# V stage of the expert layer: token-major products, the residual added by identity products

## The chip, the cores and the metric

One core of a Trainium2 chip runs the whole program. The metric is the device time of one execution in microseconds (us), and the number given for a kernel is the median of its runs. One execution is also recorded by the hardware profiler; its span runs from the first to the last instruction on the core.

## The reference

One inference step of one trunk layer, for 512 prompt tokens (with 16 meta tokens ahead of them) and 64 sample tokens: token mixers, then a layer of single-neuron experts (PEER), then a final norm. The part that matters here:

```python
qh = jnp.einsum('td,de->te', xb, w_query).reshape(PEER_BLOCK, PEER_HEADS, 2, KEY_HALF)
s = jnp.einsum('thpd,hpnd->thpn', qh, sub_keys).astype(jnp.float32)
...
gate = jax.nn.softmax(top_s, axis=-1).astype(xb.dtype)
act = jax.nn.gelu(jnp.einsum('thkd,td->thk', expert_u[eidx], xb), approximate=False)
return jnp.einsum('thk,thkd->td', gate * act, expert_v[eidx])
...
h = h + peer(rms_norm(h, norm_ffn), ...)
y = rms_norm(h, norm_final)
```

D = 1024 features, 128 x 128 = 16384 experts, 8 heads, 16 experts for each head and token.

## The kernel before

The program has three long parts: the token mixers (to about 680 us), the routing and the **U stage** (`scored`, `hidden`), and the **V stage** (`experts`). Of the 576 tokens, the last 192 are served by gathers (`gather_begin`, `gather`: GpSimd fetches one row of U or V for each of 128 tokens, VectorE takes the dot product or adds the weighted row). The first `ND` = 384 tokens are served densely: every expert is computed for them. The gathers run through the U stage and most of the V stage, in the same program order as the dense work.

The dense work goes by **halves**. A half is 128 experts. For each one SyncE loads a 512 KB tile of weights (`fetch`, seven halves ahead), ScalarE makes its rounded copy (`hi`, three halves ahead, tiles `uh`), VectorE the remainder (`lo`, two halves ahead, tiles `ul`), and TensorE makes three products per 128 x 128 block (`mm3`: rounded by rounded, rounded weights by remainder, remainder by rounded). In the U stage the product goes through Gelu and most of it is spilled to memory (`gz`). In the V stage two halves (one k) are prepared together, one k ahead: VectorE multiplies the reloaded `gz` by the gate weights `wj` (L1494), ScalarE rounds it (`ah`, L1496), and one half later VectorE makes the remainder (`al`, L1501, called from `run_due`). SyncE also loads `gz` three k ahead and `wj` in slices (`gates`).

The V stage has 128 halves. In one half TensorE takes the eight blocks d of 128 output features in turn. For a block the stationary operand is a 128 x 128 piece of the weights and the moving one is `ah` or `al`, 384 tokens wide, so the output is **feature-major**: eight banks `py[d]`, 128 features x 384 tokens (L1522 and L1523), 24 matmuls of 384 columns in a half. The order of instructions on TensorE, VectorE, ScalarE and SyncE is the order of the program from L1259 on (`in_order`).

After the first 32 halves of the V stage, which use hidden tiles kept in SBUF, the final gain (`gf`) and the residual (`yr`, eight tiles of 128 features x 384 tokens) are loaded (L1542 to L1544). The last two halves run block by block (L1551 to L1554). Behind each block VectorE adds the residual (L1555), ScalarE squares (L1558), VectorE sums the squares (L1557). Then comes the final norm: products with a column of ones (L1564) give the sum over features for each token, `rms_cols` gives the inverse root and spreads it over the partitions by products (L217), ScalarE copies it (L1567), six blocks are scaled by VectorE (L1575) and two by ScalarE and GpSimd (L1572, L1573), and eight stores of 128 rows go out from SyncE and ScalarE (L1576). Gathered tokens are normed token-major in `gather_out` and stored to `yg`.

Of the kernel before, what the change touches and what calls it, by code (L numbers as in the profile page):

```python
# [22 lines left out]
P = 128  # L23
# [25 lines left out]
NG = P + NX  # L49
ND = NT - NG  # L50
SEGD = [(0, ND)]
HB = PH // XG
TBLK = [(ND - P, P), (0, P), (P, P)]
# [67 lines left out]
class Net:  # L121
# [108 lines left out]
    def build(self):  # L230
        tc, nc, I, O = self.tc, self.nc, self.I, self.O
        self.right = ExitStack()
        with self.pool("const") as cp, self.pool("wraw", 3) as self.wraw, self.pool("whl", 2) as self.whl, \
# [5 lines left out]
            self.yd = self.dp.tile([P, KC, ND], F32, name="yd")  # L239
# [5 lines left out]
            with self.pool("y") as yp:  # L245
# [4 lines left out]
                with self.pool("x2") as xp:  # L250
                    self.x2h = [xp.tile([P, ND], F32R, name=f"x2h{k}") for k in range(KC)]
                    self.x2l = [xp.tile([P, ND], F32R, name=f"x2l{k}") for k in range(KC)]
# [664 lines left out]
    def merge(self):  # L917
# [3 lines left out]
        with self.pool("mg") as mp, self.pool("mw", 2) as wp, \  # L921
# [34 lines left out]
            for k in range(KC):  # L956
                nc.sync.dma_start(self.yd[:, k, :], self.y[k][:, :ND])
# [11 lines left out]
    def ffn_sink(self, o, w, ps, wp):  # L969
# [5 lines left out]
        def sink(k, t):  # L975
# [3 lines left out]
            else:  # L979
                self.split(self.xg[0][k], self.xg[1][k], t)  # L980
                for d, v in ((self.x2h, self.xg[0]), (self.x2l, self.xg[1])):
                    nc.sync.dma_start(d[k][:, o:].bitcast(F32), v[k][:, :ND - o].bitcast(F32))
                for x, (dst, v, a) in enumerate(((self.xt, t, w - NG), (self.yt, self.y[k], ND))):
# [30 lines left out]
    def scored(self):  # L1014
# [4 lines left out]
        self.blks = [(NT - P, P), (ND, NX)] + TBLK  # L1019
# [13 lines left out]
        self.ijg = rp.tile([P, 3, ND], F16, name="ijg")  # L1033
        self.glo = rp.tile([P, ND], F32, name="glo")
# [298 lines left out]
    def gather_out(self):  # L1333
# [8 lines left out]
        for z, (y, n, o) in enumerate(((y0, P, NX), (y1[:NX], NX, 0))):  # L1342
# [10 lines left out]
            nc.sync.dma_start(self.O["yg"][o:o + n], t)  # L1353
# [47 lines left out]
    def fetchz(self, k):  # L1401

        if NP + KEEP // 2 <= k < 2 * NP:
            z = self.zs[k] = self.zp.tile([P, 2, ND], F32, name="gz", tag="gz")
# [13 lines left out]
    def hidden(self):  # L1418
# [3 lines left out]
        self.wd = self.dp.tile([ND // TB, P, NK, TB], F32, name="wd")  # L1422
        self.gz = [self.dp.tile([P, 2, ND], F32, name=f"gz{j}") for j in range(NP - KEEP // 2)]
# [7 lines left out]
        for k in range(NP):  # L1431
# [7 lines left out]
            z = self.kp.tile([P, 2, ND], F32, name=f"gk{k}") if k >= NP - KEEP // 2 + 3 else self.zp.tile([P, 2, ND], F32, name="gz", tag="gz")  # L1439
            if kept:  # L1440
                self.zs[k + KEEP // 2] = z
            for h in range(2):
# [3 lines left out]
                for c in range(KC):  # L1446
                    self.mm3(p[:, :ND], wh[:, c, :], wl[:, c, :], self.x2h[c][:, :ND], self.x2l[c][:, :ND], c == 0, c == KC - 1)
# [4 lines left out]
                todo = (z[:, h], p[:, :ND])  # L1452
# [16 lines left out]
    def gates(self, s):  # L1469
# [4 lines left out]
        if p == 0:  # L1474
            self.wj.append(self.wjp.tile([P, ND // TB, JG, TB], F32, name="wj", tag="wj")) if g else None
            if g == 0:
                self.wj = [self.wjp.tile([P, ND // TB, JG, TB], F32, name="wj", tag="wj")]
        b, j = p * WB, (g * JG - KEEP) % NK
        m = min(WB, ND // TB - b)
# [185 lines left out]
```

## Time and profile before

| | us |
|---|---|
| median of 3 runs | 1996.18 |
| lowest and highest run | 1994.39, 2000.45 |
| the profiled execution | 1997.74 |
| its span, first to last instruction | 1996.0 |

| engine | busy us | share of the span |
|---|---|---|
| TensorE, matmul | 1917.5 | 96% |
| VectorE | 1605.4 | 80% |
| ScalarE | 910.9 | 46% |
| GpSimd | 750.1 | 38% |

The mean granted clock of TensorE is 0.984 of 2.4 GHz. The program moves 548 MB by DMA, 275 GB/s over the whole span. Matmuls are pipelined: a 384-column matmul is recorded as about 340 ns, while the next one starts about 173 ns behind it, so the busy share of TensorE is read from starts, not from durations. Busy shares are averages over stages with different limits, so the V stage (from 1412.7 us) and the time behind its last product are read by themselves.

### The profile page before, as it was taken

The numbers are of one execution on the slowest core, as the hardware profiler recorded it, in microseconds if no ns is written. First come the engines' busy times: TensorE is split into PE (matmuls) and PEld (weight loads), VectorE is DVE, ScalarE is ACT, GpSimd is POOL, SyncE is SP. The second block draws the span as 40 slices with busy tenths as digits, with TensorE's granted clock in tenths as the row PEclk, the third lists the DMA queues.
The fourth block names the chain that finished last, engine by engine and source line by source line (L and its number), as shares of the span: only waits on it lengthen the run. The fifth ranks groups of instructions, "written<-read, shape, count | busy, mean of one in ns | idle before, by whom it ended". The sixth has DMA issues, their size and how long they took to land.

```text
span 1996.0 us, 33789 instructions
## 1 busy us (share of the span) xinstructions
PE 1917.5 (96%) x12681; PEld 1849.1 (93%) x12681; DVE 1605.4 (80%) x3012; ACT 910.9 (46%) x1595; POOL 750.1 (38%) x547
## 2 busy tenths in 40 slices
PE   7999999999999898899999999999999999999997
PEld 7998999888999798899999999999999999998997
DVE  5685666667555679999999998788999798889895
ACT  5542333343323545444776899633333333333332
POOL 1110000201001355434343453366677565656530
PEclk9998999999999999999999999999999999999998
DMA  7354333464645634699899999999999999999991
GB/s 245 110 158 128 102 90 102 123 187 143 212 146 169 196 118 128 231 329 332 319 352 342 373 407 371 374 390 396 401 400 400 396 401 401 400 401 400 401 357 56
DMA packets 219905, 548.22 MB, mean 275 GB/s; under 512 B 31332, under 2 KB 96612, under 8 KB 218076
## 3 DMA queue, kind: packets, MB, share of 16 engines
q1 hardware_dynamic: 163724, 343.90, 48.9%
q0 software_dynamic: 55296, 201.35, 26.1%
q8 instruction: 99, 1.62, 0.3%
q10 hardware_dynamic: 720, 0.80, 0.1%
q14 instruction: 66, 0.54, 0.1%
HBM read 474.89 MB, written 69.77 MB: 273 GB/s over the span
## 4 chain that ended last, share of the span: by engine, by line
PE 32%; DMA 20%; DVE 5%; issue 2%; POOL 0%; ACT 0%; POOLq 0%; DVEq 0%; SPq 0%; ACTq 0%
DMA wr<-in_v 7%; PE pz L137 6%; PE pz L139 6%; PE pz L138 6%; DMA gz<-gz 5%; DMA gr<-in_v,gi 4%; PE py L138 4%; PE py L139 4%; PE py L137 4%; PE pw L1240 2%; DMA wj<-wd 2%; DVE ul L1416 1%; DMA gr<-in_ur,gi 1%; DVE gr L1322 1%; DVE yt L1329 1%
## 5 line engine op out<-in xcount | busy, mean ns | idle before, releaser
L1310 POOL DMA_INDIRECT gr<-in_ur,gi x192 | 307.7, 1603 | 271.4 <-DVE yt L1329 195.4
L1410 ACT ACTIVATE uh<-wr 128x1024 fp32r<-128x1024 f32 x256 | 270.5, 1057 | 239.1 <-PE py L138 118.0
L1310 POOL DMA_INDIRECT gr<-in_v,gi x192 | 286.0, 1490 | 242.0 <-DVE gr L1322 178.9
L138 PE MATMUL py<-al,uh 128*128 128x384 f32 x1024 | 349.1, 341 | 18.4 <-DVE al L1501 18.2
L137 PE MATMUL py<-ah,uh 128*128 128x384 f32 x1024 | 348.2, 340 | 2.3 <-ACT ah L1496 1.8
L139 PE MATMUL py<-ah,ul 128*128 128x384 f32 x1024 | 347.8, 340 | 0.0
L137 PE MATMUL pz<-x2h,uh 128*128 128x384 f32 x1024 | 346.7, 339 | 0.0
L139 PE MATMUL pz<-x2h,ul 128*128 128x384 f32 x1024 | 342.9, 335 | 2.2 <-DVE ul L1416 2.1
L138 PE MATMUL pz<-x2l,uh 128*128 128x384 f32 x1024 | 342.4, 334 | 0.0
L1416 DVE TENSOR_TENSOR ul<-wr,uh 128x1024 fp32r<-128x1024 f32 x256 | 311.6, 1217 | 15.5 <-issue 4.8
L1329 DVE SCALAR_TENSOR_TENSOR yt<-gr,ga,yt 128x1024 f32<-128x1024 f32 x192 | 245.6, 1279 | 18.7 <-DMA gr<-in_v,gi 17.7
L137 PE MATMUL acc<-xnh,wh 128*128 128x296 f32 (+1 forms) x768 | 233.4, 304 | 7.3 <-ACT xnh L296 6.2
L1322 DVE SCALAR_TENSOR_TENSOR gr<-gr,xt 128x1024 f32<-128x1024 f32 x192 | 233.3, 1217 | 5.6 <-DMA gr<-in_ur,gi 5.3
L138 PE MATMUL acc<-xnl,wh 128*128 128x296 f32 (+1 forms) x768 | 233.6, 304 | 0.5 <-DVE xnl L297 0.5
L139 PE MATMUL acc<-xnh,wl 128*128 128x296 f32 (+1 forms) x768 | 232.8, 304 | 0.4 <-DVE wl L133 0.4
L138 PEld LDWEIGHTS py<-al,uh 128*128 128x128 f32 x1024 | 195.0, 190 | 21.8 <-DVE al L1501 21.5
L132 ACT ACTIVATE wh<-wr 128x1024 fp32r<-128x1024 f32 x104 | 109.9, 1058 | 212.5 <-issue 74.0
L137 PEld LDWEIGHTS py<-ah,uh 128*128 128x128 f32 x1024 | 194.9, 190 | 3.8 <-ACT ah L1496 2.9
L139 PEld LDWEIGHTS pz<-x2h,ul 128*128 128x128 f32 x1024 | 192.2, 188 | 3.4 <-DVE ul L1416 3.4
L139 PEld LDWEIGHTS py<-ah,ul 128*128 128x128 f32 x1024 | 194.8, 190 | 0.0
L137 PEld LDWEIGHTS pz<-x2h,uh 128*128 128x128 f32 x1024 | 192.3, 188 | 0.1
L138 PEld LDWEIGHTS pz<-x2l,uh 128*128 128x128 f32 x1024 | 192.4, 188 | 0.0
(427 smaller groups left out, 3559.1 us busy)
## 6 DMA issues: line engine op xcount, KB each, us to landing
wr<-in_u SPq DMA_DIRECT2D x128, 512.0 KB, 7.2
wr<-in_v SPq DMA_DIRECT2D x128, 512.0 KB, 13.2
gz<-gz SPq DMA_DIRECT2D x96, 384.0 KB, 9.8
wr<-in_w_in SPq DMA_DIRECT2D x48, 512.0 KB, 4.0
wd<-wst SPq DMA_DIRECT2D x12, 2048.0 KB, 8.0
wj<-wd SPq DMA_DIRECT2D x96, 256.0 KB, 16.3
wr<-in_w_q SPq DMA_DIRECT2D x32, 512.0 KB, 4.2
wr<-in_w_out SPq DMA_DIRECT2D x16, 512.0 KB, 4.4
```

What stands on the lines that cost most here:

```text
L132: self.last_hi = self.nc.scalar.activation(hi, src, AF.Copy)
L137: mm(out, wh, xh, start=start, stop=False)
L138: mm(out, wh, xl, start=False, stop=False)
L139: self.last_mm = mm(out, wl, xh, start=False, stop=stop)
L1240: nc.tensor.matmul(pw[:, u, :], oh[0][:, t], oh[2 + x][:, t], start=x == 0, stop=x == 1)
L1310: nc.gpsimd.indirect_dma_start(out=t, out_offset=None, in_=src, in_offset=bass.IndirectOffsetOnAxis(ap=self.gi[z][:, x, c:c + 1], axis=0))
L1322: nc.vector.scalar_tensor_tensor(t, t, 1.0, xt, op0=ALU.mult, op1=ALU.mult, accum_out=ga[:, c:c + 1])
L1329: nc.vector.scalar_tensor_tensor(yt, t, ga[:, c:c + 1], yt, op0=ALU.mult, op1=ALU.add)
L1410: self.nc.scalar.activation(w, self.raws[s], AF.Copy)
L1416: self.nc.vector.tensor_sub(w, self.raws.pop(s), self.ws[s][0].bitcast(F32))
```

## The change

The V stage becomes **token-major**. The 384 tokens are three blocks b of 128. The stationary operand is now a 128 x 128 piece of `ah` or `al` (128 experts x 128 tokens), and the moving one is half of the weight tile, 512 output features. The output is 128 tokens x 1024 features in two banks for each block, six banks in all, and a half has 3 x 2 x 3 = 18 matmuls of 512 columns. Within a half all products of `ah` with the rounded weights come first, then those of `ah` with the remainder of the weights, then those of `al`.

The residual is added on TensorE: in eight halves (the 41st to the 48th of the V stage) three products each have a piece of `yr` stationary and the identity moving, so that the piece is transposed into the accumulating bank. The last two halves run block by block of tokens. For each block ScalarE squares both banks with the sum along the row, VectorE makes the inverse root of one column, scales the two halves by it and by `gf`, and each half is stored by itself. The tail's sums of squares, ones products, spreading and GpSimd's two scalings are gone.

The names of sizes change: `MD` = 384 takes the place of the old `ND` everywhere in the code, while `ND` becomes 1 and `NG` 575, which leaves the output `y` with one token and puts 575 in `yg`. So the first token's row of 1024 goes to `y` in its old layout (feature p of block k at [p, k, 0]), the other 127 rows of the first block go to `yg`, and the other two blocks are stored whole.

```diff
-            py = [yps.tile([P, 512], F32, name=f"py{d}") for d in range(KC)]
-            py = py[4:] + py[:4]
+            py = [yps.tile([P, 2, 512], F32, name=f"py{b}") for b in range(nb + 1)]
+            py = py[2:] + py[1:2]
...
+            def products(b, a, w, start=False, stop=False):
+                for c in range(2):
+                    nc.tensor.matmul(py[b][:, c, :], a[:, b * P:(b + 1) * P], w[:, 4 * c:4 * c + 4, :], start=start, stop=stop)
...
                     if k < 2 * NP - 1:
-                        for d in range(KC):
-                            self.mm3(py[d][:, :ND], wh[:, d, :], wl[:, d, :], ah[:, h], al[:, h], self.half == NK, False)
+                        for b in range(nb):
+                            products(b, ah[:, h], wh, start=s == NK)
+                        for b in range(nb):
+                            products(b, ah[:, h], wl)
+                        for b in range(nb):
+                            products(b, al[:, h], wh)
+                    d = s - NK - KEEP - 8
+                    if 0 <= d < KC:
+                        for b in range(nb):
+                            nc.tensor.matmul(py[b][:, d // 4, d % 4 * P:(d % 4 + 1) * P], self.y[d][:, b * P:(b + 1) * P], self.c("ident"),
+                                             start=False, stop=False)
...
+            for b in range(nb):
                 for h in range(2):
+                    wh, wl = self.ws[last - 1 + h]
+                    products(b, ah[:, h], wh)
+                    products(b, ah[:, h], wl)
+                    products(b, al[:, h], wh, stop=h == 1)
+                o = wp.tile([P, D], F32, name="yo", tag="yo", bufs=2)
+                v = wp.tile([P, 1], F32, name="yv", tag="yv", bufs=2)
+                nc.scalar.activation(o, py[b].rearrange("p a b -> p (a b)"), AF.Square, accum_out=v)
+                nc.vector.tensor_scalar(v, v, 1.0 / D, EPS, op0=ALU.mult, op1=ALU.add)
+                self.rsqrt(v, wp, bufs=2)
+                for c in range(2):
+                    sl = slice(c * 512, (c + 1) * 512)
+                    nc.vector.scalar_tensor_tensor(o[:, sl], py[b][:, c, :], v, self.gf[:, sl], op0=ALU.mult, op1=ALU.mult)
+                    if b:
+                        (nc.scalar if c else nc.sync).dma_start(self.O["yg"][b * P - ND:(b + 1) * P - ND, sl], o[:, sl])
+                    else:
+                        nc.sync.dma_start(self.O["yg"][:P - ND, sl], o[ND:, sl])
+                        nc.sync.dma_start(self.O["y"][:, 4 * c:4 * c + 4, :].rearrange("p k a -> a k p"),
+                                          o[:ND, sl].rearrange("a (k p) -> a k p", p=P))
```

## Rows read from the trace of the kernel before

**Rows 1.** The page's slices: GB/s moved, span in 40 equal slices.

```profile
GB/s 245 110 158 128 102 90 102 123 187 143 212 146 169 196 118 128 231 329 332 319 352 342 373 407 371 374 390 396 401 400 400 396 401 401 400 401 400 401 357 56
```

**Rows 2.** Busy time by stretch: PE, PEld, DVE, ACT, POOL, clock, DMA share, GB/s.

```profile
1400.00:1500.00 100.00, 98.15 (x564) 97.25 (x563) 98.53 (x114) 35.19 (x39) 70.61 (x42) 1.00 1.04 401
...
1800.00:1900.00 100.00, 93.28 (x528) 91.61 (x528) 89.09 (x102) 31.71 (x34) 60.40 (x39) 1.00 1.03 400
1900.00:1960.00 60.00, 57.99 (x325) 57.99 (x326) 55.14 (x63) 23.22 (x25) 14.82 (x9) 0.97 0.80 291
```

**Rows 3.** Groups of instructions, 1400 to 1960 us: busy, mean ns, idle before.

```profile
L138 PE MATMUL py<-al,uh 128*128 128x384 f32 x989 | 337.3, 341 | 18.4 <-DVE al L1501 18.2
```

**Rows 4.** The page's DMA issues: KB each, median us from issue to landing.

```profile
wr<-in_u SPq DMA_DIRECT2D x128, 512.0 KB, 7.2
wr<-in_v SPq DMA_DIRECT2D x128, 512.0 KB, 13.2
```

**Rows 5.** Order of time, TensorE, from 1898 us: start, duration, instruction, idle.

```profile
1898.50 0.44 PE L137 MATMUL py<-ah,uh 128*128 128x384 f32 x1 [0.50 <-ACT ah L1496]
1902.01 0.45 PE L138 MATMUL py<-al,uh 128*128 128x384 f32 x1 [3.06 <-DVE al L1501]
```

**Rows 6.** Order of time, VectorE, from 1896 us.

```profile
1896.48 0.96 DVE L1494 TENSOR_TENSOR gz<-gz,wj 128x768 f32<-128x768 f32 x1 [3.60 <-DMA gz<-gz]
...
1905.05 0.96 DVE L1494 TENSOR_TENSOR gz<-gz,wj 128x768 f32<-128x768 f32 x1 [0.77 <-DMA wj<-wd]
...
1918.62 0.95 DVE L1501 TENSOR_TENSOR al<-gz,ah 128x768 fp32r<-128x768 f32 x1
```

**Rows 7.** Order of time, TensorE: first and eleventh matmul of 256 columns.

```profile
591.72 0.28 PE L137 MATMUL pbr<-oh,wh 128*128 128x256 f32 x1
...
592.92 0.28 PE L138 MATMUL pbr<-ol,wh 128*128 128x256 f32 x1
```

**Rows 8.** The same for 384 columns, first and 26th, last whole half.

```profile
1966.80 0.34 PE L139 MATMUL py<-ah,ul 128*128 128x384 f32 x1
...
1971.13 0.34 PE L137 MATMUL py<-ah,uh 128*128 128x384 f32 x1
```

**Rows 9.** The same, four plain fp32 products of 128 columns (eight records).

```profile
228.84 1.06 PE L658 MATMUL px<-Z,Y 128*128 128x128 f32 x8
```

**Rows 10.** Order of time, all engines, last product to the last stores.

```profile
1978.24 0.34 PE L139 MATMUL py<-ah,ul 128*128 128x384 f32 x1
...
1981.22 0.16 DVE L214 TENSOR_SCALAR rmsr<-py 128x3 f32<-128x3 f32 x1 [1.59 <-PE py L1564]
...
1982.46 0.16 DVE L163 TENSOR_TENSOR rmsr<-rsq,rst 128x3 f32<-128x3 f32 x1
...
1984.89 3.24 DVE L1575 SCALAR_TENSOR_TENSOR yo<-yr,par,py 128x384 f32<-128x384 f32 x6 [2.26 <-ACT rb L1567]
1985.53 4.54 SPq L1576 DMA_DIRECT2D out_y<-yo  x4
```

**Rows 11.** The chain that ended last, its last piece: start, us, what.

```profile
1988.68 1.03 POOLq L1661
```

**Rows 12.** The square with row sum in the first norm: ns min, median, max.

```profile
L307 ACT ACTIVATE xt<-xt x5: 1059/1060/1061, 13.5 to 21.9; 128x1024 f32<-128x1024 f32 x4, 80x1024 f32<-80x1024 f32 x1
L307 ACT ACTIVATION_READ_ACCUMULATOR xt<-xt x5: 183/186/189, 14.4 to 22.9; 128x1 f32 x4, 80x1 f32 x1
```

**Rows 13.** DMA in 75.9 to 76.3 us: 40 slices, packets, one small store.

```profile
GB/s 0 0 0 0 0 0 0 0 0 0 0 0 0 0 1 1 1 1 1 1 1 1 1 1 1 1 1 1 0 0 0 0 0 0 0 0 0 0 0 0
DMA packets 36, 0.00 MB, mean 0 GB/s; under 512 B 36, under 2 KB 36, under 8 KB 36
```

**Rows 14.** DMA in 1978 to 1996 us: 40 slices, packets, landing of stores.

```profile
GB/s 0 0 0 0 0 0 0 0 0 0 0 0 0 0 0 0 0 0 123 348 369 376 96 242 355 372 359 362 380 120 14 0 0 0 0 0 0 0 0 0
DMA packets 1153, 1.58 MB, mean 88 GB/s; under 512 B 128, under 2 KB 1152, under 8 KB 1152
...
out_y<-yo ACTq DMA_DIRECT2D x4, 192.0 KB, 1.9
```

More of the change, by code (lines that the diff above doesn't have):

```diff
@@ L250, in build @@
                 with self.pool("x2") as xp:
-                    self.x2h = [xp.tile([P, ND], F32R, name=f"x2h{k}") for k in range(KC)]
-                    self.x2l = [xp.tile([P, ND], F32R, name=f"x2l{k}") for k in range(KC)]
+                    self.x2h = [xp.tile([P, MD], F32R, name=f"x2h{k}") for k in range(KC)]
+                    self.x2l = [xp.tile([P, MD], F32R, name=f"x2l{k}") for k in range(KC)]
                     with self.pool("x2g") as gp:
@@ L1421, in hidden @@
         tc, nc, I = self.tc, self.nc, self.I
-        self.wd = self.dp.tile([ND // TB, P, NK, TB], F32, name="wd")
-        self.gz = [self.dp.tile([P, 2, ND], F32, name=f"gz{j}") for j in range(NP - KEEP // 2)]
+        self.wd = self.dp.tile([MD // TB, P, NK, TB], F32, name="wd")
+        self.gz = [self.dp.tile([P, 2, MD], F32, name=f"gz{j}") for j in range(NP - KEEP // 2)]
         self.gdone, self.gcred, self.gready = 0, 0.0, True
@@ L1438, in hidden @@
             kept = k >= NP - KEEP // 2
[L1439 removed]
+            z = self.kp.tile([P, 2, MD], F32, name=f"gk{k}") if k >= NP - KEEP // 2 + 3 else self.zp.tile([P, 2, MD], F32, name="gz", tag="gz")
             if kept:
@@ L1540, in experts @@
                     self.gf = wp.tile([P, D], F32, name="gf")
-                    self.y = [wp.tile([P, ND], F32, name=f"yr{k}") for k in range(KC)]
+                    self.y = [wp.tile([P, MD], F32, name=f"yr{k}") for k in range(KC)]
                     nc.sync.dma_start(self.gf, I["gain"].to_broadcast([P, D]))
@@ L1560, in experts @@
-            col, t = py[0][:, :nb], py[1][:, :ND]
-            w = [min(P, ND - b * P) for b in range(nb)]
-            for b in range(nb):
-                for x in (0, KC - 1):
-                    nc.tensor.matmul(col[:w[b], b:b + 1], sq[x][:, b * P:b * P + w[b]], self.c("ones")[:, :1], start=x == 0, stop=x > 0)
-            rs = self.rms_cols(col, t, w, wp)
-            rb = wp.tile([P, ND], F32, name="rb")
-            nc.scalar.activation(rb, rs, AF.Copy)
-            for k in range(KC):
-                g = self.p("norm_final")[:, k:k + 1]
-                o = wp.tile([P, ND], F32, name="yo", bufs=KC)
-                if k in (2, 6):
-                    nc.scalar.activation(o, self.y[k], AF.Copy, scale=g)
-                    nc.gpsimd.tensor_mul(o, o, rb)
-                else:
-                    nc.vector.scalar_tensor_tensor(o, self.y[k], g, rs, op0=ALU.mult, op1=ALU.mult)
-                (nc.scalar if k % 2 else nc.sync).dma_start(self.O["y"][:, k, :], o)
+                    wh, wl = self.ws[last - 1 + h]
```

64 lines of the change are left out of this document (28 added, 36 removed).

## The prediction, written before the changed kernel was run

> **What bounds the kernel now.** I read the GB/s slices of the page first, then the table by stretch, then the idle time of the V stage's groups, then the order of time at the end of that stage and behind it.
>
> The GB/s slices stand at 390 to 401 from about 1250 us to about 1900 us, and nowhere above 407 [rows 1]. In 1400 to 1500 and 1800 to 1900 us the DMA share is over 1.0 [rows 2], so the transfers are at their ceiling whatever the engines do. TensorE is busy 98 and then 93 of 100 us there, so it waits a little. Its largest idle group in the V stage is 18.4 us, ended by VectorE's `al` [rows 3], and VectorE itself is held by loads: 3.60 us for `gz`, 0.77 us for `wj` [rows 6]. A weight tile lands 13.2 us behind its issue in the V stage, 7.2 us in the U stage [rows 4]: a queue of transfers stands there all the time. So **the V stage up to about 1900 us is bound by DMA**, and TensorE follows.
>
> The last such wait is seen at 1898.50 to 1902.01, 3.06 us on `al` behind one single matmul of the half [rows 5]. Behind that the gathers run out (DMA share 0.80 in 1900 to 1960 [rows 2]), and TensorE runs on without a wait to its last product, which starts at 1978.24 and ends at 1978.6 [rows 10]. **From there to the end of the span (1996.0) are 17.4 us of tail.**
>
> **The products, half by half.** Eleven matmuls of 256 columns start within 1.20 us, 0.120 each [rows 7]; 26 of 384 columns within 4.33 us, 0.173 each [rows 8]. The line through both is 0.0416 us for 100 columns on a fixed part of 0.0134, so 512 columns give 0.2264 us, an estimate from these two. A half then takes 18 x 0.2264 = 4.08 us in place of 24 x 0.173 = 4.16: 0.08 us saved, 10.6 us over 128 halves if TensorE set the pace. It doesn't up to 1900 us, since the bytes stay the same and the ceiling holds. I put the saving there at nothing; the cover is the DMA queue, and without it the saving would be the 10.6 us and up to the 18.4 us of idle.
>
> **The order within a half.** Today the second matmul of a half needs `al`. Afterwards 12 of 18 come first, 12 x 0.2264 = 2.7 us, so TensorE may run that far ahead of `al`. In the DMA-bound part this gains nothing that lasts. At its end it does, once. VectorE's own order isn't touched; from 1905.05 it runs without a gap that a load causes. I take its `al` times as they are and ask which one ends last. For the `al` that is complete at 1918.62 + 0.95 = 1919.57 [rows 6], 14 halves are left (1978.6 - 14 x 4.16 = 1920.4, where its first product stands today). Afterwards 6 matmuls of its half are still to come, then 18, then 6 x 36 = 240 in all, 54.3 us: the last product ends at **E = 1973.9**. The `al` of 1902.0, one pair more and another behind it, would give 1972.7. So E comes 4.7 us earlier; bounds are 1.1 (only 14 x 0.08 saved, if something else holds the order) and 6.
>
> **The residual.** 24 fp32 products of 128 columns. Four such took 1.06 us [rows 9], so 24 take 6.4 us, 0.8 us in each of eight halves at about 1590 to 1625 us. (The stage's mean half is (1978.6 - 1412.7) / 128 = 4.42 us, and these are the halves from the 41st on.) TensorE is idle 2 to 7% there [rows 2], 0.1 to 0.3 us a half, gets 0.08 from the wider matmuls, and falls back about 0.5 us a half, 4 us in all; it then has over 60 halves behind a full DMA queue to make it up. The cost is nothing, and 4 us if the queue ran dry. The products add a wait on TensorE for `yr`, with all its later matmuls queued behind; but `yr` is asked for nine halves, 40 us, earlier, three times the 13.2 us of a load [rows 4]. VectorE's eight additions leave the tail. The loads of `yr` are where they were.
>
> **The new tail, block by block.** Three blocks end at E - 5.43, E - 2.72 and E (12 matmuls for each block, 2.72 us). The chain of the first block: square with row sum 1.06 + 0.19 [rows 12], there from SBUF, here from PSUM; from the first step of the inverse root to its end 1.40 (1981.22 to 1982.62) [rows 10]; scaling of 512 columns, from 3.24 us for six of 384 [rows 10] 0.54 each, or 0.72 for 512, taken as 0.8 with its start. The first half of block 0 is ready at E - 1.9, the second at E - 1.1. SyncE issues it within 0.1 us; its bytes move 0.6 to 1.0 us later (issue 1985.53 [rows 10], first bytes in the nineteenth slice of 0.45 us [rows 14]): **E - 1.0.**
>
> Here stands the point on which the time hangs: **the stores of 127 rows.** A store of 128 rows has 16 completion writes (8 stores, 128 packets under 512 B [rows 14]), one for each of the 16 engines that share it. The store of 4 rows at 76 us, 32 elements of 4 bytes, shows 36 packets [rows 13], so 4 completions and 4 engines. The rows were shared in equal parts each time. 127 rows have no equal parts but 1 or 127. Read so, all 127 go to one engine; read as "as many engines as rows, up to 16", they go to all. The nearest bounds are these: spread, 260 KB at 400 GB/s take 0.65 us; on one engine, at a sixteenth of 401 GB/s [rows 2], 25.1 GB/s, they take 10.4 us. I take the second, because every store in the trace has equal parts. There are two of these, on one queue and so one behind the other: 20.8 us.
>
> The Trainium skill, "DMA: Bandwidth & Descriptors", section "Why a DMA increments its semaphore by 16 and not by 1", says that a transfer uses the largest number up to 16 that divides the slowest dimension of both sides, and names 127 partitions as an example that ends on one engine. By that rule the sum is the one below; by the other reading it is the first rival's; no run here shows it yet.
>
> Between them lie the two stores of token 0, 512 elements of 4 bytes each, scattered. The 36 packets above took about 0.15 us on 4 engines [rows 13], 17 ns each on an engine; 128 on each of four engines are 2.2 us, twice 4.4 (bounds 2 and 13, for the scattered addresses). The other two blocks bring four stores of 256 KB, each 0.65 us on the same engine: 2.6. **Sum on that engine 20.8 + 4.4 + 2.6 = 27.8, ending at E + 26.8.** Blocks 1 and 2 are long done by then.
>
> **The close.** Today the last bytes move in the slice that ends at 1991.95 [rows 14], 4.0 us before the end; the chain ends on GpSimd's closing instruction [rows 11], behind its two products, which go. I take 1.5, bounds 0.5 and 4.
>
> Span after: 1973.9 + 26.8 + 1.5 = 2002.2, against 1996.0: **6.2 us more**. The profiled execution took 1997.74, 1.7 outside its span and 1.6 above the median of the three runs; on that median of 1996.18 the forecast is **2002.4**. Alone, this case spans 1997 to 2011: 0 to 6 us at E, 2.5 at the close, 9 in the small elements, and a long run of one engine may go slower than its share of 16.
>
> **Rivals.**
> *The 127 rows are spread, chance 0.14.* Then the tail is the chain of the last block. ScalarE issues the second store of block 1 only behind its scaling, at E + 1.6, and the square of block 2 stands behind that: 1.9 + 1.25 + 1.4 + 1.6 = E + 6.2, 1.9 us to landing [rows 14], 1.0 to close: 1983.0, 13 us less, 1983.2 on the median. This decides for faster; the point is one number, the engines of a 127-row store. For it: no such count is in the trace. Against: equal parts.
> *One engine each, but not the same one, 0.04.* The two run side by side, each E - 1.0 + 10.4, with one small store and the shares of blocks 1 and 2 behind it (2.2 + 2.6) and the close: E + 15.7, 1989.6, 6.4 us less than before, about 1989.8 on the median.
> *TensorE set the pace after all, 0.06.* Then part of the 10.6 and 18.4 us comes out of the V stage, say half beside the long store: 1988. Against it stands 401 GB/s without a dip [rows 1, 2].
> *The order does nothing at the end, within the first case:* E stays near 1977, time near 2006.
>
> **How the numbers follow.** Forecast case 0.76, rivals 0.14, 0.04, 0.06. A difference under 0.3%, 6.0 us, can't be told from none. The forecast case lies just over that line; I give 0.45 of its 0.76 to slower, 0.29 to the same, 0.02 to faster. With the rivals: faster 0.26, same 0.29, slower 0.45. The range leaves out 0.1 at the top and under the spread case: 1981.5 to 2011; the forecast case's own is 1997 to 2011.
>
> **What would show it.** Matmuls of 512 columns should start 0.226 us apart. The GB/s slices should stand at 400 as long as before, and the V stage's last product should end near 1974 of the span, with waits on `al` shorter. Behind it the GB/s should fall to about 25 for some 20 us: one engine at work, no compute. If GB/s is high and the end comes within 10 us of the last product, the 127 rows were spread and the forecast is wrong. If the last product comes before 1970, the reading of the V stage as DMA-bound is wrong.

## The result, and the profile after

The changed kernel takes **2010.21 us** (median of 5 runs, 2007.25 to 2014.98) against 1997.73 for the kernel before beside it: a ratio of 1.0065, 95% interval 1.0044 to 1.0085, so it is slower by 0.65%. The forecast was 2002.4 us, in a range of 1981.5 to 2011.0, with slower as the likeliest case; the loss, 12.5 us, is twice the 6.2 us forecast. The profiled execution of the changed kernel took 2007.25 us, its span is 2005.4.

Three pieces of the span are told apart below: up to the first product of the V stage, from there to the end of the last product (E, as in the prediction), and the tail behind E. Each row has one profiled execution; E is the start of the last group of products plus its duration.

| kernel | V stage from | E | V stage | span | tail |
|---|---|---|---|---|---|
| before | 1412.7 | 1978.6 | 565.9 | 1996.0 | 17.4 |
| changed | 1408.5 | 1972.6 | 564.1 | 2005.4 | 32.8 |

The part ahead of the V stage is the same work in both; over all the kernels below it ends between 1406.3 and 1414.4, with no order that follows an edit. So the lengths of the V stage and of the tail are compared, and not E itself. The tail got 15.4 us longer, the V stage 1.8 us shorter. The second figure rests on one execution of each, and kernels with one and the same V stage differ by as much (563.3 to 565.1 below).

The page's GB/s slices of the changed kernel, 40 equal slices of the span:

```profile
GB/s 254 116 155 119 95 92 99 135 173 164 206 156 149 199 127 155 244 326 330 332 355 321 391 402 372 381 388 395 399 401 399 400 401 401 401 400 400 401 265 32
```

The ceiling of 400 stands as long as before [rows 1]; the last two slices, 265 and 32, are below the 357 and 56 of before. The same by stretch (busy us of PE, PEld, DVE, ACT, POOL, then granted clock, DMA share, GB/s):

```profile
1400.00:1500.00 100.00, 97.83 (x427) 79.35 (x427) 99.51 (x115) 34.82 (x38) 70.68 (x43) 1.00 1.03 400
1800.00:1900.00 100.00, 94.13 (x398) 73.91 (x397) 88.81 (x100) 32.08 (x34) 61.44 (x38) 1.00 1.03 401
1900.00:1960.00 60.00, 58.15 (x247) 45.61 (x246) 53.16 (x62) 22.54 (x25) 9.73 (x6) 1.00 0.71 256
1977.00:1990.00 13.00, 0.00 (x0) 0.00 (x0) 0.00 (x0) 0.00 (x0) 0.00 (x0) 0.50 0.10 22
```

The first three answer [rows 2]: still 400 GB/s. The fourth is new: 13 us in which no engine computes and 22 GB/s move. The DMA view of 1970 to 2005.4 us in 40 slices of 0.885 us shows it closer:

```profile
GB/s 0 7 19 9 19 185 141 28 24 21 25 25 25 25 25 12 9 16 9 21 26 36 26 25 25 21 25 25 25 14 250 46 0 0 0 0 116 380 97 0
DMA packets 1865, 1.58 MB, mean 45 GB/s; under 512 B 1098, under 2 KB 1098, under 8 KB 1864
```

The slices of about 25 are a sixteenth of 401 GB/s, in two long stretches, as forecast; before, the stores of the tail ran at 242 to 380 GB/s in most of their slices [rows 14]. The 250 behind the slow stretch (1996.6 to 1997.4 us) is block 1's first store, which stood behind block 0's on SyncE. Then there are four empty slices and a burst, block 2's stores. The order of time from the first store on (start, duration, engine or queue, line, tile; in brackets the idle time before it and what ended it) says why:

```profile
1969.66 1.41 DVE L1579 SCALAR_TENSOR_TENSOR yo<-py,yv,gf 128x512 f32<-128x512 f32 x2
1970.47 0.27 SPq L1584 DMA_DIRECT2D out_yg<-yo  x1
1970.79 3.99 SPq L1585 DMA_DIRECT2D out_y<-yo  x1
1971.98 0.63 PE L1522 MATMUL py<-uh,al 128*128 128x512 f32 x2
1974.89 9.01 SPq L1584 DMA_DIRECT2D out_yg<-yo  x1
1983.94 3.93 SPq L1585 DMA_DIRECT2D out_y<-yo  x1
1988.31 13.66 SPq L1581 DMA_DIRECT2D out_yg<-yo  x2
1998.18 1.02 ACT L1574 ACTIVATE yo<-py 128x1024 f32<-128x1024 f32 x1 [26.80 <-DMA out_y<-yo]
2000.80 1.41 DVE L1579 SCALAR_TENSOR_TENSOR yo<-py,yv,gf 128x512 f32<-128x512 f32 x2
2002.30 0.34 ACTq L1581 DMA_DIRECT2D out_yg<-yo  x1
```

Block 2's products are done at 1972.6, but its square starts at 1998.18, 25.6 us later (ScalarE had stood idle for 26.80 us), released by the store `out_y<-yo` of block 0. The square writes `yo`, the tile has two buffers, and block 2 gets that of block 0, which is still being read by the slow stores. Behind it stands the rest of the chain and the store of block 2, 7.2 us to the end of the span. The chain that ended last has the same steps:

```profile
1974.89 9.01 SPq L1584
1983.94 14.09 DMA out_y<-yo
1998.18 1.12 ACT yo L1574 x2
2000.80 0.75 DVE yo L1579
2001.55 0.66 DVEq L1671
```

### The profile page after: what moved, and what is told of

It is laid out like the page before. It is cut to its first block, busy times and chain, and to the rows that moved or that the text cites. A ratio compares the mean times of both kernels' runs of the same rounds, so it can differ in the third digit from the quotient of the medians.

```text
span 2005.4 us, 32314 instructions
## 1 busy us (share of the span) xinstructions
PE 1915.2 (96%) x11943; PEld 1737.3 (87%) x11943; DVE 1600.5 (80%) x3010; ACT 907.6 (45%) x1592; POOL 746.1 (37%) x545
## 4 chain that ended last, share of the span: by engine, by line
PE 30%; DMA 22%; DVE 5%; issue 2%; POOL 1%; SPq 1%; ACT 0%; DVEq 0%; POOLq 0%; ACTq 0%
DMA wr<-in_v 9%; PE py L1522 7%; PE pz L138 7%; PE pz L140 7%; PE pz L139 7%; DMA wj<-wd 4%; DMA gr<-in_v,gi 3%; DMA gz<-gz 2%; PE pw L1241 2%; DVE ul L1417 1%; DMA gr<-in_ur,gi 1%; DVE yt L1330 1%; POOL gr L1311 1%; DMA out_y<-yo 1%; DVE gr L1323 1%
## 5 line engine op out<-in xcount | busy, mean ns | idle before, releaser
L1330 DVE SCALAR_TENSOR_TENSOR yt<-gr,ga,yt 128x1024 f32<-128x1024 f32 x192 | 245.8, 1280 | 16.6 <-DMA gr<-in_v,gi 15.6
L1522 PE MATMUL py<-ul,ah 128*128 128x512 f32 x768 | 202.8, 398 | 8.2 <-DVE ul L1417 8.2
L1522 PE MATMUL py<-uh,ah 128*128 128x512 f32 x768 | 201.9, 397 | 6.8 <-ACT ah L1497 6.2
L1522 PE MATMUL py<-uh,al 128*128 128x512 f32 x768 | 200.5, 395 | 0.0
L1522 PEld LDWEIGHTS py<-ul,ah 128*128 128x128 f32 x768 | 142.4, 188 | 49.9 <-DVE ul L1417 16.9
L1522 PEld LDWEIGHTS py<-uh,ah 128*128 128x128 f32 x768 | 143.0, 188 | 43.5 <-ACT ah L1497 9.0
L1522 PEld LDWEIGHTS py<-uh,al 128*128 128x128 f32 x768 | 144.2, 188 | 35.1
```

What stands on the lines that cost most here:

```text
L1330: nc.vector.scalar_tensor_tensor(yt, t, ga[:, c:c + 1], yt, op0=ALU.mult, op1=ALU.add)
L1522: nc.tensor.matmul(py[b][:, c, :], a[:, b * P:(b + 1) * P], w[:, 4 * c:4 * c + 4, :], start=start, stop=stop)
```

## The experiments

Theory: the whole loss lies in the form in which block 0 is stored (127 rows on one engine, 1024 single elements) and in the buffer that it holds; the V stage follows its transfers, so the new order there gains a few us at its end. Against it: the new products, their order or the identity products cost time; or 127 rows are slow for another reason. Each V stage and tail of the table is that of one profiled execution; a dash stands where there is no ratio beside it. Four kernels leave a part of the work out: no_elem and rows122 store 8 of token 0's 1024 elements, no_al lacks the products with `al` (but for the last two halves), no_ident lacks the residual.

| kernel | V stage from | E | V stage | span | tail | ratio to before, 95% |
|---|---|---|---|---|---|---|
| bufs3 | 1414.4 | 1978.4 | 564.0 | 2006.4 | 28.0 | 1.0045 (1.0031 to 1.0059) |
| no_elem | 1413.3 | 1976.6 | 563.3 | 2005.5 | 28.9 | - |
| rows122 | 1410.8 | 1975.9 | 565.1 | 1995.0 | 19.1 | - |
| rows112 | 1406.8 | 1970.7 | 563.9 | 1987.9 | 17.2 | 0.9978 (0.9961 to 0.9994) |
| rows112_bufs3 | 1411.4 | 1975.1 | 563.7 | 1988.3 | 13.2 | 0.9977 (0.9962 to 0.9992) |
| whole | 1407.6 | 1971.0 | 563.4 | 1980.6 | 9.6 | 0.9944 (0.9926 to 0.9962) |
| best | 1406.3 | 1970.0 | 563.7 | 1977.3 | 7.3 | 0.9918 (0.9893 to 0.9944) |
| ul_last | 1410.1 | 1975.5 | 565.4 | 1982.9 | 7.4 | 0.9937 (0.9916 to 0.9958) |
| same_bank | 1414.2 | 1982.5 | 568.3 | 2015.2 | 32.7 | - |
| no_al | 1409.8 | 1967.9 | 558.1 | 2000.5 | 32.6 | - |
| no_ident | 1412.7 | 1976.6 | 563.9 | 2009.4 | 32.8 | - |
| before_al_last | 1410.7 | 1976.0 | 565.3 | 1992.7 | 16.7 | 1.0006 (0.9993 to 1.0019) |

**bufs3**: what the buffer costs.

```diff
-o = wp.tile([P, D], F32, name="yo", tag="yo", bufs=2)
-v = wp.tile([P, 1], F32, name="yv", tag="yv", bufs=2)
+o = wp.tile([P, D], F32, name="yo", tag="yo", bufs=3)
+v = wp.tile([P, 1], F32, name="yv", tag="yv", bufs=3)
```

> The changed kernel with three buffers in place of two for the output tile yo and its column yv, nothing else. In the changed kernel's trace the square of block 2 stands 26.8 us behind the stores of block 0, since it writes the buffer that they read, and starts only at 1998.18; the chain and the store behind it end the span 7.2 us later. Theory (the reuse of the buffer is a part of the tail of its own): block 2's square starts within 3 us of the last product, its stores leave before or beside the long ones, and the span ends about 1.5 to 2.5 us behind the last bytes of block 0 at 1998.0: about 2000, 5 to 6 us less than the changed kernel's 2005.4, still slower than before by 0.1 to 0.4%. Rival (the buffer is only what the profile names; the queue of stores on the one engine sets the end anyway): block 2's stores land behind those of block 0 on the same engine, and the span stays within 2 us of 2005.4.

The tail is 28.0 instead of 32.8: **4.8 us**, a little under the 5 to 6 of the theory; the ratio falls from 1.0065 to 1.0045, but its interval overlaps that of the changed kernel, so the trace shows this and not the ratio. Block 2's square starts 1.7 us behind E. Its wait is no longer ended by the stores of block 0, but by VectorE's scaling of block 1, which ScalarE's own store of that block waits for:

```profile
1980.12 1.02 ACT L1574 ACTIVATE yo<-py 128x1024 f32<-128x1024 f32 x1 [2.95 <-DVE yo L1579]
```

The rest of the tail is the slow stores and what stands behind them on SyncE.

**no_elem**: what the 1024 single elements cost.

```diff
-nc.sync.dma_start(self.O["y"][:, 4 * c:4 * c + 4, :].rearrange("p k a -> a k p"),
-                  o[:ND, sl].rearrange("a (k p) -> a k p", p=P))
+nc.sync.dma_start(self.O["y"].rearrange("p k a -> a k p")[:, 4 * c:4 * c + 1, :4],
+                  o[:ND, sl].rearrange("a (k p) -> a k p", p=P)[:, :1, :4])
```

> The changed kernel whose two stores of token 0 move 4 elements each in place of 512 (the rest of token 0 is left out of the output); the two stores of 127 rows and the two buffers stay. Theory (127 rows go to one engine, 25 GB/s, and are slow by themselves): two times 10.4 us from about 1.0 us before the last product, so block 0's last bytes stand at E + 20, block 2's square there, the end 7.3 us later: span E + 27 against E + 32.8 in the changed kernel; the 5 to 6 us between are the price of the 1024 elements. Rival (the scattered elements, with 3.9 to 4.0 us on SyncE for the issue of each, are what holds the queue, and the rows behind them only wait): the rows land 2 us behind their issue, the span ends at E + 10.

The tail is 28.9: the elements cost **3.9 us**, somewhat less than expected here and near the 4.4 of the prediction. The rest stays. SyncE's queue in order of time:

```profile
1974.48 0.27 SPq L1584 DMA_DIRECT2D out_yg<-yo  x1
1974.81 4.00 SPq L1585 DMA_DIRECT2D out_y<-yo  x1
1978.92 0.77 SPq L1584 DMA_DIRECT2D out_yg<-yo  x1
1979.73 7.90 SPq L1585 DMA_DIRECT2D out_y<-yo  x1
```

A store of four elements takes SyncE 4.00 and 7.90 us to issue, at least as long as one of 512 did (3.99 and 3.93). So the elements are not what makes the issue long: the long row store in front is. The expectation of rows112, written before this was seen, had that wrong.

**rows112**: the same rows in two stores with other counts.

```diff
-nc.sync.dma_start(self.O["yg"][:P - ND, sl], o[ND:, sl])
+nc.sync.dma_start(self.O["yg"][:P - 16, sl], o[ND:P - 15, sl])
+nc.sync.dma_start(self.O["yg"][P - 16:P - ND, sl], o[P - 15:, sl])
```

> The changed kernel with block 0's store of 127 rows written as two stores, 112 rows and 15 rows, both halves of the columns; the two scattered stores of token 0 stay as they are, and the buffers too. Theory (127 rows go to one engine because they have no equal parts): 112 rows go to 16 engines, 15 rows to 15; the stretch of 25 GB/s goes. SyncE still spends 4.0 us on issuing each scattered store (seen at 1970.79), so block 0 is done about 1970.5 + 0.6 + 4.0 + 0.6 + 4.0 + 2 = 1981.7, block 2's square starts there, and the span ends 7.2 us later at about 1989: 16 us less than the changed kernel, 7 less than the kernel before (faster by 0.3%). Rival A (the stores are slow because they start at partition 1, or because of the scattered stores between them): 112 rows from the same partition 1 are as slow, the span stays near 2005. Rival B (spread over all 16 engines in any case, the slices of 25 GB/s come from the 4-byte stores alone): the same, near 2005.

The tail is 17.2 instead of 32.8: **15.6 us** come back (16 expected), and the ratio, 0.9978, lies below 1. The start at partition 1 and the elements are as they were, so neither made the rows slow. Order of time:

```profile
1969.42 0.74 SPq L1586 DMA_DIRECT2D out_y<-yo  x1
1972.94 0.93 SPq L1586 DMA_DIRECT2D out_y<-yo  x1
1980.75 1.02 ACT L1574 ACTIVATE yo<-py 128x1024 f32<-128x1024 f32 x1 [11.30 <-DMA out_y<-yo]
```

The expectation was right for the rows, wrong for a part of the way: the issue of 512 elements takes 0.74 and 0.93 us, not 4.0, but they are slow to land: the second is issued at 1972.94, and block 2's square waits for it until 1980.75.

**rows122**: the rule of equal parts, with a count whose largest divisor up to 16 is 2.

```diff
+# on top of no_elem
-nc.sync.dma_start(self.O["yg"][:P - ND, sl], o[ND:, sl])
+nc.sync.dma_start(self.O["yg"][:P - 6, sl], o[ND:P - 5, sl])
+nc.sync.dma_start(self.O["yg"][P - 6:P - ND, sl], o[P - 5:, sl])
```

> As the kernel with 4 elements of token 0 in each scattered store, but the 127 rows are written as 122 rows and 5 rows. Theory (a store is shared in equal parts by the largest number of engines up to 16 that divides its rows): 122 is 2 x 61, so two engines, 61 rows of 2 KB each; at 25 GB/s on an engine that is 5.0 us in place of 10.4, two of them 10.0; block 0's last bytes at about E + 9.5, span about E + 17, and slices of about 50 GB/s. Rival A (only a multiple of 16 rows is shared, all else goes to one engine): 25 GB/s, 10.0 us each, span about E + 26. Rival B (any store of 16 rows and more goes to 16 engines, 127 is slow for another reason): span about E + 10.

The GB/s of 1970 to 1995 us, 40 slices:

```profile
GB/s 0 0 0 0 0 0 0 26 26 33 26 46 49 82 259 184 108 252 118 66 56 46 52 52 52 52 46 49 3 0 0 0 0 0 0 164 374 302 0 0
```

They stand at 46 to 52, **twice those of 127 rows**, and the tail is 19.1 (17 expected; 26 if it were one engine, 10 if all). That is two shares at 25 GB/s each: the rows go in equal parts to the largest number of engines up to 16 that divides them, and for 127, a prime, that is one. By the rule of the Trainium skill ("DMA: Bandwidth & Descriptors", section "Why a DMA increments its semaphore by 16 and not by 1") 127 rows get one engine, 122 two and 112 sixteen; with 25, about 50 GB/s and no long stretch the three kernels agree.

**whole** and **best**: token 0 stays in the token-major output. In best there are also three buffers, and every store goes out from SyncE.

```diff
-ND, NG = 1, NT - 1
+ND, NG = 0, NT
...
+(nc.scalar if c and b else nc.sync).dma_start(self.O["yg"][b * P:(b + 1) * P, sl], o[:, sl])   # whole
+nc.sync.dma_start(self.O["yg"][b * P:(b + 1) * P, sl], o[:, sl])   # best, with bufs=3
```

> The changed kernel with token 0 kept in the token-major output: block 0 is stored as 128 rows, the scattered stores and the output y in feature-major form go; two buffers as in the changed kernel. Theory (all of the loss is in the form of block 0's stores): each store of 128 rows has landed some 2 us behind its issue, block 0's about 1974; block 2's square stands behind ScalarE's own store of block 1 (about 1974.3) and no more behind a buffer; chain 4.1 us to the end of the scaling, 2 us to landing, 1 to close: span about 1982, E + 9, some 23 us less than the changed kernel and 14 less than the kernel before (ratio 0.993). Rival (the V stage in its new order is itself slower, by wider matmuls or by the identity products): E comes no earlier than the 1978.6 of the kernel before and the time is within 0.3% of it or above.

> As the kernel with token 0 kept in the token-major output, with three buffers for yo and yv, and all six stores from SyncE, so that ScalarE's square of block 2 waits for neither a buffer nor ScalarE's own issue of a store. Theory: the square of block 2 starts within 0.3 us of the last product instead of about 1.7 behind it; the span ends about 1.6 us earlier than with the whole rows alone, about 1980.5, 15 us less than before. Rival (SyncE's issues, one behind the other, or the landing of the stores set the end): no difference from the kernel with whole rows alone, within 0.5 us.

With whole rows the tail is **9.6 us**, 23.2 less than in the changed kernel and 7.8 less than before. This is the tail that the prediction's first rival worked out for spread rows (E + 9.1). In best, block 2's square waits for TensorE alone:

```profile
1970.01 1.02 ACT L1574 ACTIVATE yo<-py 128x1024 f32<-128x1024 f32 x1 [1.26 <-PE py L1522]
```

best takes another 2.3 off and has a tail of 7.3, where 1.6 less was expected for buffer and queue together; what each of the two is worth was not tried alone. With a median of 1980.2 us against 1998.2 for before beside it, best is the fastest kernel of this study, ratio 0.9918.

**rows112_bufs3**: the smallest mend that keeps the output's form.

> The kernel with block 0's rows stored as 112 and 15, its two scattered stores kept, and three buffers for yo and yv. In the kernel with 112 and 15 rows and two buffers the span ended at E + 17.2 (E 1970.7, the end of the last product), and block 2's square still stood 11.3 us behind a scattered store, to E + 10.0. Theory (the 1024 elements hold that buffer, the rest is chain): with a buffer of its own block 2 is scaled by E + 6.2, its stores go out behind the scattered ones on SyncE's queue, the end comes about 2 us behind their last landing at E + 10: span E + 12, about 5 us less than with two buffers, while token 0 keeps its output. Rival (SyncE's queue is held by the scattered stores so that block 2's store lands no earlier): E + 16 or more.

The edits are those of rows112 and bufs3 together. The tail is 13.2 (12 expected, 16 or more by the rival), 4.0 less than with two buffers. The two ratios, 0.9977 and 0.9978, can't show that: their intervals are 3 us wide to either side, and this profiled V stage began 4.6 us later. Against whole rows 3.6 us remain; what differs are the scattered elements and the stores of 15 rows, beside the third buffer; which of them holds the 3.6 us was not tried alone.

**no_al**: what bounds the V stage.

```diff
-for b in range(nb):
-    products(b, al[:, h], wh)
```

> The changed kernel without the products of the activations' low part with the weights in the V stage (6 of the 18 of a half; they stay in the last pair), so part of the sum is left out; VectorE still makes the low part. Theory (the V stage follows the transfers until about 1900 us): TensorE has 1.4 us less to do in each of 126 halves, 176 us in all, but only what it does behind the last transfers gets shorter, at most the 14 halves or so behind 1913, 20 us: the V stage takes 540 to 560 us in place of 564.1, the GB/s slices stay at 400 as long as before, and TensorE's idle time takes up the rest. Rival (TensorE sets the pace of the V stage, 97 to 100 of 100 us busy): the V stage gets some 150 us or more shorter.

A third of TensorE's products of the V stage is gone, about 176 us of work, and the stage gets **6.0 us** shorter (558.1). By stretch:

```profile
1400.00:1500.00 100.00, 82.25 (x333) 58.99 (x331) 98.54 (x113) 35.45 (x41) 69.68 (x42) 1.00 1.03 400
1800.00:1900.00 100.00, 71.19 (x261) 48.99 (x261) 89.09 (x101) 31.91 (x35) 61.13 (x39) 0.97 1.03 399
1900.00:1960.00 60.00, 47.75 (x182) 33.76 (x181) 54.72 (x63) 23.17 (x26) 12.31 (x7) 0.97 0.74 267
```

TensorE is busy 71 to 82 of 100 us, and DMA stands at 399 to 400 GB/s as ever. So TensorE, though busy 94 to 98 of 100 us in these stretches of the changed kernel, doesn't set the length of the stage.

It does set the pace at first. In the changed kernel TensorE waits 0.6 us in all up to 1560 us, and a half takes 4.20 us, the price of its 18 products; in the kernel before it takes 4.16, in no_al 3.9. Counted from the first product of the stage, the 37th half starts at 151.3 us in the changed kernel, at 150.2 before and at 140.2 in no_al. The 61st starts at 257.4, 262.7 and 256.6, in the same order: no_al's lead of 11 us is gone. At the 121st (528.7 in the changed kernel, 527.5 in no_al) the lead is 1.2 us, and the other 4.8 come in the last halves, behind the transfers.

VectorE is busy 89 to 99 of 100 us beside it, and could be the limit too. Its idle time in 1400 to 1900 us of the changed kernel is 45 us, and 39 of them are ended by two loads (us in total, times, longest):

```profile
DVE gz L1495 <- DMA wj<-wd: 21.7, 8, 4.6
DVE gz L1495 <- DMA gz<-gz: 17.3, 7, 3.9
```

In no_al the same two waits are 20.7 and 21.8 us. So VectorE follows the transfers as well. No run gave VectorE less work, so how far its own work adds to the length isn't shown.

**no_ident**: the residual's price.

```diff
-if 0 <= d < KC:
-    for b in range(nb):
-        nc.tensor.matmul(py[b][:, d // 4, d % 4 * P:(d % 4 + 1) * P], self.y[d][:, b * P:(b + 1) * P], self.c("ident"), ...)
```

> The changed kernel without the 24 identity products that add the residual (the residual is left out of the sum); its loads stay. Theory (the 24 products lie in the part of the V stage that waits for transfers): the V stage stays within 0.7 us of 564.1. Rival (TensorE is busy 100 of 100 us in that stretch and does not make up for them): 24 products of 128 columns, two records of about 0.11 us each, 5 to 6.4 us less.

The V stage takes 563.9 us without the 24 products and 564.1 with them: in the end they cost nothing that can be told, as forecast, though TensorE has no idle time in the 100 us of the changed kernel in which the first of them stand:

```profile
1500.00:1600.00 100.00, 100.00 (x443) 81.00 (x442) 89.91 (x104) 33.89 (x36) 60.97 (x39) 1.00 1.04 400
```

There they do push TensorE back:

```profile
1580.83 0.83 PE L1540 MATMUL py<-cst,yr 128*128 128x128 f32 x6
1585.69 0.83 PE L1540 MATMUL py<-cst,yr 128*128 128x128 f32 x6
```

The halves stand 4.86 us apart, 0.66 more than without them. The 49th half starts 5.3 us later than in no_ident (207.0 and 201.7 us from the first product), and by the 61st that is made up (257.4 and 258.3).

**same_bank** and **ul_last**: the order of a half, and the length of a 512-column product. same_bank takes the three products of a bank one behind the other; ul_last, on top of best, swaps the two last groups.

```diff
+# same_bank, in place of the three loops over products
+for b in range(nb):
+    for c in range(2):
+        for a, m in ((ah, wh), (ah, wl), (al, wh)):
+            nc.tensor.matmul(py[b][:, c, :], a[:, h, b * P:(b + 1) * P], m[:, 4 * c:4 * c + 4, :], ...)
```

```diff
 # ul_last
-for b in range(nb):
-    products(b, ah[:, h], wl)
 for b in range(nb):
     products(b, al[:, h], wh)
+for b in range(nb):
+    products(b, ah[:, h], wl)
```

> The changed kernel with another order of the same 18 products in a half: for each of the six banks its three products (hi x hi, hi x lo, lo x hi) one behind the other, so that the bank changes at every third matmul and the low part of the activations is needed at the third matmul of a half instead of the thirteenth. Theory (a 512-column product costs 0.233 us whatever bank the one before wrote, and the V stage waits for transfers): the period stays 0.233; the V stage, 564.1 us in the changed kernel from its first to its last product, comes back to some 565 to 567 us, since the low part is waited for earlier in the half. Rival (the change of bank at each matmul is what makes a 512-column product 0.007 us longer than the line through the shorter ones says): the period falls to about 0.228 and the V stage to 562 or less.

> The kernel with whole rows of block 0, three buffers and all stores from SyncE, with one edit in the V stage: the products of the activations' low part come second and those of the weights' low part ul last, so that ul is needed at the thirteenth matmul of a half and al at the seventh. In the kernels with al last the last waits of TensorE are on ul (1.32 us at 1944.34 in the changed kernel, 1.06 and 0.95 us at 1902 and 1912 in this one's base). Theory (ul is next to be late when al is not): the waits on ul go, al is early enough at the seventh matmul, and the V stage gets 0.5 to 1.5 us shorter than the 563.7 us of its base. Rival (al is the later of the two again, as with al at the third matmul, where the V stage took 568.3): the V stage gets longer, 564 to 567.

In same_bank the 23rd product starts at 1902.87, the first at 1897.73:

```profile
1897.73 0.39 PE L1533 MATMUL py<-ul,ah 128*128 128x512 f32 x1
1902.87 0.39 PE L1533 MATMUL py<-uh,al 128*128 128x512 f32 x1
```

That is 5.14 us for 22 steps, 0.2336 each, so the change of bank is not what makes these products longer than extrapolated, and that rival falls. The V stage takes 568.3 us where `al` is needed at the third product of a half, 565.4 where at the seventh, and 563.3 to 565.1 where at the thirteenth, in eight kernels. In ul_last my theory fell: with `al` at the seventh the last waits are on `al` again.

```profile
1898.05 1.67 PE L1522 MATMUL py<-uh,al 128*128 128x512 f32 x6 [1.84 <-DVE al L1502]
1907.60 1.67 PE L1522 MATMUL py<-uh,al 128*128 128x512 f32 x6 [0.88 <-DVE al L1502]
1917.88 1.67 PE L1522 MATMUL py<-uh,al 128*128 128x512 f32 x6 [1.62 <-DVE al L1502]
```

So the order of the change is better than `al` at the third product, by some 4 us in one execution (in which the granted clock also stood at 0.50 for 3.4 us at 1914.3). Against `al` at the seventh the gain is not shown: 565.4 lies 0.3 us above the eight, and the intervals of the two ratios, best and ul_last, overlap.

**before_al_last**: the order alone, in the old form.

```diff
-for d in range(KC):
-    self.mm3(py[d][:, :ND], wh[:, d, :], wl[:, d, :], ah[:, h], al[:, h], self.half == NK, False)
+for x, (m, a) in enumerate(((wh, ah), (wl, ah), (wh, al))):
+    for d in range(KC):
+        nc.tensor.matmul(py[d][:, :ND], m[:, d, :], a[:, h], start=self.half == NK and x == 0, stop=False)
```

> The kernel before with one edit, the order of the 24 products in a half of the V stage: first hi x hi for all eight banks, then the weights' low part with hi, then hi with the activations' low part, so that the low part of the activations is needed at the seventeenth of 24 matmuls instead of the second. Feature-major products, 384 columns, residual, norm and stores as before. Theory (the order alone brings TensorE's work forward where the transfers run out, and nothing up to there): the V stage gets 2 to 5 us shorter than its 565.9 us, the span likewise, ratio 0.9975 to 0.999, hard to tell from no change. Rival A (the order frees TensorE in the whole stage, the 18.4 us that it stands idle for the low part): 10 to 18 us less, ratio 0.991 to 0.995. Rival B (the order does nothing, another operand is late at the same places): V stage within 1 us of 565.9.

The ratio is 1.0006 (0.9993 to 1.0019) and the V stage 0.6 us shorter, less than the spread between kernels with one and the same V stage. The order alone gives nothing that can be told here; rival B holds. The last wait of TensorE isn't on `al` any more, but it is there:

```profile
1906.04 2.92 PE L1524 MATMUL py<-ah,uh 128*128 128x384 f32 x8 [2.18 <-ACT ah L1496]
```

The last wait, 3.06 us on `al` [rows 5], has become one of 2.18 us on `ah`.

## Why the prediction was right, and where not

Two errors add up. The tail is 32.8 us, where the steps gave 28.3 (2002.2 - 1973.9): 4.5 us. The V stage got 1.8 us shorter, where 4.7 were counted: 2.9 us. Together they are 7.4 us, and the median stands 7.8 above the forecast, near the upper end of the range. That the two agree so well is partly luck: the profiled V stage began 4.2 us earlier than before, so its span is only 3.2 us above the 2002.2, and this execution is the fastest of the five.

**127 rows on one engine: right.** The stores move at 25 GB/s, and the rows122 and rows112 kernels show that equal parts are the reason. This was the point on which sign and size hung; storing the rows as 112 and 15 takes 15.6 us off the tail.

**The sum on that engine: right in total.** It was to end at E + 26.8; block 0's last store lands and frees block 2's square at 1998.18, E + 25.6. The elements, 4.4, measured 3.9.

**"Blocks 1 and 2 are long done by then": this is the step that failed.** Block 1's chain is, but its first store stands on SyncE behind block 0's and moves at 1996.6. Block 2 needs the buffer of block 0, and the line that says so, bufs=2, stood in the change. So the end isn't a close of 1.5 us behind the last bytes of block 0, but the square, root, scaling and store of block 2, 7.2 us. The error of 5.7 is softened by the 1.2 that the stores ended earlier. bufs3 gives 4.8 back and so shows the mechanism; its tail of 28.0 is close to the 28.3 that the steps gave. In the rival with spread rows I had ScalarE's queue hold that square, but never asked for the buffer.

**512 columns in 0.2264 us: too short.** The first products of three groups of six:

```profile
1898.22 1.56 PE L1522 MATMUL py<-uh,ah 128*128 128x512 f32 x6
1899.62 1.56 PE L1522 MATMUL py<-ul,ah 128*128 128x512 f32 x6
1901.02 1.56 PE L1522 MATMUL py<-uh,al 128*128 128x512 f32 x6
```

Six take 1.40 us, 0.2333 each. A half is 4.20 us and not 4.08, so it isn't shorter than the 4.16 of before [rows 8]. The line through 256 and 384 columns doesn't reach to 512; why isn't known, only that it isn't the change of bank (same_bank).

**The V stage bound by transfers: right for its length**, by no_al and the standing 400 GB/s. In the first 36 halves TensorE sets the pace, and what it loses or gains there is evened out later. (The slices of 390 and more begin at about 1297 us, not 1250 [rows 1]; nothing hangs on that.) Its idle groups in 1400 to 1960 us (busy us and mean ns, then idle before) answer [rows 3]:

```profile
L1522 PE MATMUL py<-ul,ah 128*128 128x512 f32 x750 | 197.5, 398 | 8.2 <-DVE ul L1417 8.2
L1522 PE MATMUL py<-uh,ah 128*128 128x512 f32 x751 | 197.0, 397 | 6.8 <-ACT ah L1497 6.2 <-ACT gk L1467 0.6
L1522 PE MATMUL py<-uh,al 128*128 128x512 f32 x750 | 195.1, 395 | 0.0
```

The 18.4 us on `al` became 8.2 us on `ul` and 6.8 us, nearly all on `ah`: the wait changed its name, and the stage nearly kept its length.

**E, 4.7 us earlier: the term was too large.** It took the times of `al` as the one limit and 14 halves of 4.08 us behind them. 14 halves of 4.20 take back 1.7 us. And `ul`, which VectorE makes in the same order, was next to be late:

```profile
1936.14 1.22 DVE L1345 TENSOR_TENSOR yt<-yt,gr 64x1024 f32<-64x1024 f32 x1 [2.04 <-DMA gr<-yt]
1943.08 1.21 DVE L1417 TENSOR_TENSOR ul<-wr,uh 128x1024 fp32r<-128x1024 f32 x1
1944.34 1.67 PE L1522 MATMUL py<-ul,ah 128*128 128x512 f32 x6 [1.32 <-DVE ul L1417]
```

VectorE waits for a reload of the gathered tokens, norms them, and comes to `ul` at 1943.08; TensorE waits 1.32 us for it. With 0.49 us more at 1913.35 that leaves 4.7 - 1.7 - 1.8 = 1.2, against 1.8 measured. This sum is argued from the trace; no run took the reload away. That VectorE "runs without a gap that a load causes" was read from too short a stretch. Already in the kernel before it waits 0.71 us for `gr` at 1940.30.

**"TensorE runs on without a wait to its last product": right, but not at full clock.** In the kernel before the granted clock stands at 0.50, the level of 1.2 GHz, for 3.4 us soon behind the wait of 3.06 us on `al` (first line: stretch, busy us, clock, DMA share, GB/s), and the products start 0.32 us apart in place of 0.173:

```profile
1903.04:1906.45 3.41, 3.41 (x12) 3.41 (x11) 2.64 (x4) 1.33 (x2) 1.67 (x1) 0.50 1.00 392
1903.60 0.52 PE L139 MATMUL py<-ah,ul 128*128 128x384 f32 x1
1903.92 0.52 PE L137 MATMUL py<-ah,uh 128*128 128x384 f32 x1
```

From 1903.00 to 1906.47 eleven products take 1.6 us more than at the upper level, in a stretch behind which TensorE has no other wait. before_al_last has such a stretch too, 1906.08 to 1909.49; in the changed kernel's V stage the clock is 1.00 throughout. So most of the 1.8 us may be the clock and not the order of the products; no run tells the two apart.

**The residual, hidden: right** (no_ident); it pushed TensorE back by 5.3 us, where about 4 were forecast, and the stage made that up. **The first store at E - 1.9:** it was issued at 1970.47, E - 2.1.

## What to carry to other kernels

Count the rows of a store before the bytes: where a block is cut by one token, 127 rows at 25 GB/s cost more here than the whole V stage's new order brought, and 112 and 15 rows, or a block kept whole, mend it. Where a tail has slow stores, ask which tile they read, how many buffers it has, and who writes it next: that writer, and all of its chain, starts behind them. When one operand's wait is moved out of the way in a stage that follows its transfers, look for the operand that is late next; the saved wait is not a gain until the length of the stage says so.

## What the hardware showed that I had not expected

The issue of a store can be long for what stands in front of it: on SyncE four elements took 4.00 us behind a one-engine store of 127 rows, and 512 elements 0.74 us where the rows were spread. One engine runs at its sixteenth: 25 GB/s, and two at about 50.

In the first 36 halves TensorE waited 0.6 us in all and set the pace, and yet a third less work for it shortened the stage by 6.0 us only: a lead of 11 us was gone 24 halves later, when the transfers set the pace.

512-column products, each with a weight load of its own, start 0.233 us apart at a granted clock of 1.00 of 2.4 GHz. That is 0.060 us more than for 384 columns, where the step from 256 to 384 costs 0.053 [rows 7, 8]. The Trainium skill, "TensorE: Matmul & The Clock Gate", section "Back-to-back issue gap", gives about 216 ns for 512 columns as the isolated gap, and about 131 ns in a stream with weight loads; the trace agrees with neither, and the 233 ns of the trace decide here.
